# Layer 0's feed forward written in program order, with one work area for several stages

## The chip, the cores and the metric

The kernel runs on one core of a Trainium2 chip. The engines are TensorE (PE: matmuls; its weight loads are shown as PEld), VectorE (DVE), ScalarE (ACT) and GpSimd (POOL); SyncE (SP) issues the DMAs from HBM. Every engine works through its own queue in order; semaphores make one engine wait for another. The metric is the device time of one execution, in microseconds: before the change it is 1958.71, the median of 3 runs that lie between 1958.17 and 1960.01.

## The reference

Two layers over 512 latent and 256 context tokens of width 1024, in fp32, cut here to what the change touches:

```python
def adaln(cond, w_mod, b_mod):
    return jnp.split(jax.nn.silu(cond) @ w_mod + b_mod, N_MOD, axis=-1)     # six vectors of 1024
def swiglu(h, w1, w3, w2):
    return (jax.nn.silu(h @ w1) * (h @ w3)) @ w2                            # D_FF = 2816
def reference(x, c, ctx, c_ctx, w_mod, ...):
    for l in range(2):
        sh1, sc1, gt1, sh2, sc2, gt2 = adaln(c, w_mod[l], b_mod[l])         # for the latent tokens
        csh1, csc1, cgt1, csh2, csc2, cgt2 = adaln(c_ctx, w_mod[l], b_mod[l])   # for the context tokens
        h = modulate(rms_norm(x, norm1[l]), sh1, sc1)
        ... attention, convolution and gMLP branches, each with a gate, summed and projected ...
        x = x + gt1 * merge_branches(...)
        x = x + gt2 * swiglu(modulate(rms_norm(x, norm2[l]), sh2, sc2), w_ff1[l], w_ff3[l], w_ff2[l])
        if l == 0: the same for ctx
    return x
```

## The kernel before

Activations lie transposed: 128 channels on the partitions, the tokens along the free dimension (768 tokens in layer 0, 512 in layer 1). An fp32 product is made of three products of a shorter type: each operand is split into a high part (ACT's cast, L242) and a low part, the difference of the two (on DVE or POOL, L243), and PE adds high x high, high x low and low x high (`mm`, L252). So each 128x512 piece of a weight matrix (256 KB, tile ws, loaded by SP) costs a cast (wh) and a subtraction (wl) before PE can use it. Raw pieces have five slots, high and low parts four each.

Layer 0's feed forward has 22 blocks of 128 hidden channels. Blocks 0 and 1 are made by `first_pair` (L1189). The other twenty are made two at a time by `ff_pair` (L1215): once for w1 (the silu product) and once for w3 (the gate product), each by `pair_product` (L342), a 2 x 2 block product with seven multiplications in place of eight. One multiplication takes one piece of weights and is 12 matmuls of 384 columns (L349). Four of the seven pieces are sums or differences of raw pieces (tile fw, L282 in `factors`), made on DVE; forms of the activations are ready in the tiles A and B. ACT copies intermediate products out of PSUM (tile tp, L358 to L367), DVE forms the outputs of the silu product (L1220 to L1227) and of the gate product (L1234 to L1247), POOL multiplies the two, and `keep_u` splits the result (tile u) for FF2.

The 22 blocks go in five parts: 4, 4, 4, 4 and 6. After each part `ff2_j` (L1270) multiplies its u tiles by eight columns of w2, 24 matmuls for each in the first four parts (512 and 256 columns in turn), and DVE adds the result, times the gate gt2, to the residual (tile xr, L1275).

In the same time DVE computes layer 1's adaln vectors, the sums: 48 pieces of w_mod (512 KB each, tile wm) are multiplied by silu(c), the first sixteen also by silu(c_ctx), and summed along the free dimension (L159). These are 64 operations of 128x1024. `pump` advances them, twice after each pair product and once after every second FF2 block; the load of each (L156) waits for a one-column copy on POOL (`bg_stage`, L183) of a value that the stage has just made, so that a load cannot start long before its stage.

The order of every queue is set by the scheduler of the tile framework, which plans with modelled times; the program's order is only its input. PSUM is used as four banks in two tiles of 1024 columns ("wide") and four single banks ("pD"). Each stage has work tiles of its own (silu output su, tp, fw, score tiles pp, gate tiles: five of 768 columns and two of 512, and others).

## Time and profile before

| | us |
|---|---|
| median of 3 runs | 1958.71 (1958.17 to 1960.01) |
| profiled execution | 1952.57 |
| its span, first to last instruction | 1950.8 |
| PE busy over the span | 1872.5 (96 %) |
| DVE / ACT / POOL busy | 1129.7 / 821.1 / 727.5 |
| PE busy, 0 to 655 us (layer 0 up to the first pair of blocks) | 610.72 |
| PE busy, 655 to 1127 us (layer 0's pairs and the FF2 of the first four parts) | 451.52 of 472.00 |
| PE busy, 1127 us to the end (last FF2 part, layer 1) | 810.27 of 823.80 |

A row of the profile names a line of the kernel, the engine, the operation and its tiles (output, arrow, inputs); x12 is a count. Rows of groups give the busy time, the mean duration in ns, and the idle time of the engine ahead of them with what ended it. In the timeline a row begins with its start and its duration in us, and square brackets hold the idle time before it. A row of waits gives who waited for whom, the total in us, how often, and the longest.

### The profile page before, as it was taken

What the parts mean: (1) busy time and instruction counts of PE and PEld (TensorE: products, weight loads), DVE (VectorE), ACT (ScalarE), POOL (GpSimd) and SP (SyncE); (2) the same over time, 40 slices, a digit from 0 to 9 for tenths busy, and PEclk for the clock granted to TensorE, in tenths of its full rate; (3) what the DMA queues carried; (4) which work ended last, traced back from release to release, by engine and by line L of the source; (5) the groups of instructions that cost most, each with busy time, mean ns of one, the idle gap of its engine ahead of it and who ended that gap; (6) DMA issues with size and microseconds to landing.
All of it is one profiled execution on the core that took longest, in us unless ns stands there. A gap on an engine that the chain in (4) does not pass through costs nothing.

```text
span 1950.8 us, 27784 instructions
## 1 busy us (share of the span) xinstructions
PE 1872.5 (96%) x10146; PEld 1643.3 (84%) x10146; DVE 1129.7 (58%) x1850; ACT 821.1 (42%) x1544; POOL 727.5 (37%) x636
## 2 busy tenths in 40 slices
PE   5999999999999998999999999999999999999999
PEld 4778889888889888888989987888788888888887
DVE  7588877684566877766666657358633461222212
ACT  3547766322225523342433446458533353223231
POOL 4434533332214233333333338654332243233231
PEclk9999999999999999999999999999999999999999
DMA  8653211443443143434343254320133433332333
GB/s 298 225 199 103 71 39 36 136 154 108 147 172 109 55 130 104 134 116 145 122 137 125 71 171 142 105 87 12 34 96 98 140 120 103 97 98 87 108 94 96
DMA packets 109449, 225.58 MB, mean 116 GB/s; under 512 B 12288, under 2 KB 21248, under 8 KB 109184
## 3 DMA queue, kind: packets, MB, share of 16 engines
q1 hardware_dynamic: 108208, 221.96, 35.2%
q10 hardware_dynamic: 1104, 1.84, 0.3%
q8 instruction: 80, 1.31, 0.3%
q14 instruction: 57, 0.47, 0.1%
HBM read 215.89 MB, written 5.24 MB: 113 GB/s over the span
## 4 chain that ended last, share of the span: by engine, by line
PE 76%; DVE 10%; DMA 4%; issue 4%; ACT 3%; POOL 2%; SPq 0%; DVEq 0%; ACTq 0%; POOLq 0%
PE wide L252 29%; PE pD L252 26%; PE pF L252 5%; PE pD L349 5%; PE wide L349 5%; PE pO L1060 2%; DMA wm<-in_w_modT 2%; DMA ws<-in_w 2%; PE wide L1028 2%; PE pPT L1054 2%; DVE wl L243 1%; DVE wm L159 1%; ACT wh L242 1%; DVE nm L1032 1%; DVE fw L282 1%
## 5 line engine op out<-in xcount | busy, mean ns | idle before, releaser
L243 POOL TENSOR_TENSOR wl<-ws,wh 128x512 fp32r<-128x512 f32 (+2 forms) x290 | 382.4, 1321 | 693.2 <-ACT wh L242 682.0
L242 ACT CAST wh<-ws 128x512 fp32r<-128x512 f32 (+2 forms) x534 | 322.4, 607 | 704.6 <-PE wide L252 249.7
L243 DVE TENSOR_TENSOR wl<-ws,wh 128x512 fp32r<-128x512 f32 x244 | 189.6, 780 | 308.2 <-ACT wh L242 305.7
L252 PE MATMUL wide<-A,wh 128*128 128x512 f32 (+2 forms) x1104 | 315.8, 374 | 14.5 <-POOL A L243 5.8
L252 PE MATMUL pD<-A,wh 128*128 128x512 f32 (+1 forms) x1184 | 324.2, 369 | 0.1
L252 PEld LDWEIGHTS wide<-A,wh 128*128 128x128 f32 x1104 | 200.1, 192 | 53.2 <-POOL A L243 7.9
L252 PEld LDWEIGHTS pD<-A,wh 128*128 128x128 f32 x1184 | 207.5, 189 | 38.1 <-POOL A L243 0.3
L252 PE MATMUL pD<-A,wl 128*128 128x512 f32 (+1 forms) x592 | 202.5, 369 | 1.3 <-POOL wl L243 1.3
L252 PE MATMUL wide<-A,wl 128*128 128x512 f32 (+2 forms) x552 | 196.2, 372 | 0.3 <-DVE wl L243 0.3
L252 PE MATMUL wide<-u,wh 128*128 128x512 f32 (+1 forms) x624 | 156.9, 353 | 0.6 <-DVE xr L1275 0.6
L159 DVE SCALAR_TENSOR_TENSOR wm<-wm,fixed 128x1024 f32<-128x1024 f32 x96 | 128.2, 1336 | 35.1 <-DMA wm<-in_w_modT 34.5
L252 PEld LDWEIGHTS pD<-A,wl 128*128 128x128 f32 x592 | 104.3, 188 | 20.7 <-POOL wl L243 2.1
L252 PEld LDWEIGHTS wide<-u,wh 128*128 128x128 f32 x624 | 104.1, 188 | 17.9 <-DVE xr L1275 1.2
L252 PEld LDWEIGHTS wide<-A,wl 128*128 128x128 f32 x552 | 101.9, 192 | 17.7 <-POOL wl L243 0.8
L252 PE MATMUL pD<-u,wh 128*128 128x512 f32 (+1 forms) x432 | 114.6, 358 | 0.0
L1037 POOL TENSOR_SCALAR pp<-pp,nm 128x768 f32<-128x768 f32 (+1 forms) x80 | 69.0, 864 | 106.7 <-DVE nm L1036 87.4
L159 DVE SCALAR_TENSOR_TENSOR junk<-wm,fixed 128x1024 f32<-128x1024 f32 x48 | 64.2, 1338 | 57.6 <-DMA wm<-in_w_modT 57.6
L252 PE MATMUL wide<-u,wl 128*128 128x512 f32 (+1 forms) x312 | 96.2, 353 | 0.1
L252 PE MATMUL pF<-A,wh 128*128 128x256 f32 (+1 forms) x384 | 94.2, 331 | 0.0
L242 ACT CAST wh<-fw 128x512 fp32r<-128x512 f32 x80 | 49.0, 619 | 95.7 <-PE wide L349 26.6
L349 PE MATMUL wide<-B,wh 128*128 128x384 f32 x320 | 81.6, 338 | 5.4 <-ACT wh L242 5.2
L252 PEld LDWEIGHTS pD<-u,wh 128*128 128x128 f32 x432 | 74.2, 188 | 12.3 <-ACT wh L242 0.2
(288 smaller groups left out, 3770.9 us busy)
## 6 DMA issues: line engine op xcount, KB each, us to landing
ws<-in_w SPq DMA_DIRECT2D x256, 256.0 KB, 2.7
wm<-in_w_modT SPq DMA_DIRECT2D x112, 512.0 KB, 4.7
ws<-in_w_in SPq DMA_DIRECT2D x184, 256.0 KB, 2.6
ws<-in_w_o SPq DMA_DIRECT2D x48, 256.0 KB, 2.6
ws<-in_w_abc SPq DMA_DIRECT2D x32, 256.0 KB, 2.6
ws<-in_w_six SPq DMA_DIRECT2D x16, 192.0 KB, 5.2
xr<-in_xT SPq DMA_DIRECT2D x8, 384.0 KB, 8.3
ws<-in_w SPq DMA_DIRECT2D x16, 192.0 KB, 2.3
```

Source lines behind the costliest of these rows:

```text
L159: nc.vector.scalar_tensor_tensor(o, t, 1.0, sbc[:, c, :], op0=ALU.mult, op1=ALU.mult, accum_out=MOD[l][:, sec, b, c:c + 1])
L242: nc.scalar.copy(hi, src)
L243: (lo_eng or nc.gpsimd).tensor_tensor(lo, src, f(hi), op=ALU.subtract)
L252: nc.tensor.matmul(d[:, :b - a], lhsT=ww, rhs=aa[:, a:b], start=kk == 0 and i == 0, stop=kk == n - 1 and i == 2)
L282: nc.vector.tensor_tensor(o, x, y, op=op)
L349: nc.tensor.matmul(D, lhsT=x[:, kk * P:(kk + 1) * P], rhs=a, start=not more and kk == 0 and i == 0, stop=kk == 3 and i == 2, skip_group_ch ...
L1028: nc.tensor.matmul(D[:, a - k0:b - k0], lhsT=q[:, c * P - q0:(c + 1) * P - q0], rhs=kt[:, a:b], start=i == 0, stop=i == 1)
L1032: nc.vector.tensor_reduce(nm[:, 0:1], D[:, :nk], axis=AX.X, op=ALU.max, negate=True)
L1037: nc.gpsimd.tensor_scalar(pt[:, :nk], pt[:, :nk], nm[:, 3:4], 0.0, op0=ALU.mult, op1=ALU.add)
L1054: nc.tensor.transpose(TD[:, (2 * j + cc) * P:(2 * j + cc + 1) * P], pts[cc][:, kc:kc + P], ident)
L1060: nc.tensor.matmul(o[:, 0:256], lhsT=v3[:, kt, :], rhs=pp[:, j * 256:(j + 1) * 256], start=gi == 0 and j == 0 and i == 0, stop=gi == len(k ...
```

## The change

`ff_layer_0` holds all of layer 0's feed forward from the second pair to the last; its body stands in `tc.manual_schedule()`, in which every queue runs in the order of the program. The first pair, the FF2 of the last part and all other stages are ordered by the scheduler as before.

- `flow` takes the place of `factors` and `taken`: one stream of pieces for pairs and FF2 alike, made three ahead of their use. A raw load is issued when the piece that last used its slot has been made. The low parts of FF2 pieces are all made on DVE; before, some of them were made on POOL.
- The sums of layer 1 come at fixed steps: at the third multiplication of each pair product (EXTRA), after the FF2 blocks 2 to 7 of the first two parts, and after every FF2 block of the next two. A sum's load is issued three steps ahead, into a ring of four, with no copy on POOL.
- `behind` delays a silu or a `keep_u` by one or two pieces in the program's order.
- FF2 of a part starts with the two older u tiles for column 0, then for column 1, then the two newer ones for both.
- PSUM is eight single banks in rotation (pE) within `ff_layer_0`.
- One tile `work` of 9472 columns holds rings for the sums, score tiles (pp), gate tiles (six), su, tp, fw and a tile of the first stage; some rings share columns. Two u tiles of each part lie in unused halves of the A tiles. Some tiles are merged or moved (q and qc, pt, wx, wb), and the homes of A and B are swapped for layer 1.

The matmuls and their number are the same (10066 instructions on PE's queue in both). DVE has 16 instructions more, POOL 64 fewer (48 of them the copies). The diff, cut to its core:

```diff
+    work = const.tile([P, 9472], F32, name="work")
+    RINGS = {"sums": (0, 1024, 4), "turned": (4096, 2560, 1), "pp": (0, 1536, 3), "gate": (4864, 768, 6),
+             "su": (4096, 768, 2), "tp": (5632, 384, 6), "fw": (7936, 512, 3)}
+    place = dict.fromkeys(RINGS, 0)
+    place["gate"] = 3
+    def area(name, n=None):
+        a, w, bufs = RINGS[name]
+        i = place[name]
+        place[name] = (i + 1) % bufs
+        return work[:, a + i * w:a + i * w + (n or w)]
...
     def wm_stage():
-        return wp.tile([P, 1024], F32, tag="wm", name="wm", bufs=3)
+        return area("sums")
+    def spare(skip=2):
+        i = (place["sums"] + skip) % 4 * 1024
+        return work[:, i:i + 1024]
...
+    ahead_sums = []
+    sums_1 = iter([(sec, b, (0, 1) if sec < 2 else (0,)) for sec in (1, 0, 2, 4, 3, 5) for b in range(KD)])
+    def load_1():
+        x = next(sums_1, None)
+        if x:
+            t = wm_stage()
+            nc.sync.dma_start(t, w_modT[1, x[0] * KD + x[1]])
+            ahead_sums.append((*x, t))
+    def sums_layer_1():
+        if ahead_sums:
+            sec, b, cs, t = ahead_sums.pop(0)
+            for c in cs:
+                o = t if c == cs[-1] else spare(0)
+                nc.vector.scalar_tensor_tensor(o, t, 1.0, sbc[:, c, :], op0=ALU.mult, op1=ALU.mult,
+                                               accum_out=MOD[1][:, sec, b, c:c + 1])
+            if b == KD - 1:
+                mod_rest(1, sec, 0, KD, 0, len(cs))
+            load_1()
...
-    def factors(srcs):
-        def load(n, b, k0):
-            if n == len(srcs):
-                return None
-            t = wtile("s")
-            nc.sync.dma_start(t, srcs[n][b][:, k0:k0 + 4, :].rearrange("p k n -> p (k n)"))
-            return t
-        def parts(x, eng=nc.vector):
-            hi, lo = wtile("h"), wtile("l")
-            split(x, hi, lo, eng)
-            return hi, lo
-        def total(x, y, op):
-            o = slot("fw", 512)
-            nc.vector.tensor_tensor(o, x, y, op=op)
-            return o
-        nxt = [load(0, *i) for i in ((0, 0), (1, 0), (1, 4), (0, 4))] + [load(1, 0, 0)]
-        for n in range(len(srcs)):
-            a11, a21, a22, a12, *nxt = nxt
-            yield parts(a11, nc.gpsimd)
-            s1 = total(a21, a22, ALU.add)
...
+    def flow(items, ahead=3):
+        n_s, loads, raw, todo = 5, [], [], []
+        def need(src, last):
+            loads.append((src, last))
+            return len(loads) - 1
+        for pair, x in items:
+            t0 = len(todo)
+            if not pair:
+                i = need(x, t0)
+                todo.append((lambda i=i: raw[i], nc.vector))
+                continue
+            a11, a21, a22, a12 = (need(x[b][:, k0:k0 + 4, :].rearrange("p k n -> p (k n)"), t0 + last)
+                                  for b, k0, last in ((0, 0, 4), (1, 0, 4), (1, 4, 6), (0, 4, 5)))
+            s = {}
+            def total(name, p, q, op, s=s):
+                def go():
+                    o = s[name] = area("fw")
+                    u, v = (raw[i] if isinstance(i, int) else s[i] for i in (p, q))
+                    nc.vector.tensor_tensor(o, u, v, op=op)
+                    return o
+                return go
+            todo += [(lambda i=a11: raw[i], nc.gpsimd), (total("s1", a21, a22, ALU.add), nc.vector),
+                     (total("s2", "s1", a11, ALU.subtract), nc.vector), (total("s4", "s2", a12, ALU.subtract), nc.vector),
+                     (total("s3", a11, a21, ALU.subtract), nc.vector), (lambda i=a12: raw[i], nc.vector),
+                     (lambda i=a22: raw[i], nc.vector)]
+        made, summed, count = [], [], [0, 0]
+        def issue():
+            while len(raw) < len(loads) and (len(raw) < n_s or loads[len(raw) - n_s][1] < count[0]):
+                t = wtile("s")
+                nc.sync.dma_start(t[:, :loads[len(raw)][0].shape[1]], loads[len(raw)][0])
+                raw.append(t)
+        def sums():
+            if count[1] < len(todo):
+                summed.append(todo[count[1]][0]())
+                count[1] += 1
+        def make():
+            if summed:
+                x, (_, eng) = summed.pop(0), todo[count[0]]
+                hi, lo = wtile("h"), wtile("l")
+                split(x, hi, lo, eng)
+                made.append((hi, lo))
+                count[0] += 1
+                issue()
+        issue()
+        sums()
+        def take(as_is=False):
+            while not as_is:
+                sums()
+                make()
+                if len(made) > ahead or not summed:
+                    break
+            for w in waiting:
+                w[0] -= 1
+            while waiting and waiting[0][0] <= 0:
+                waiting.pop(0)[1]()
+            return made.pop(0)
         return take
+    waiting = []
+    def behind(n, what):
+        waiting.append([n, what])
...
-    def pair_product(take, tmp, ev11, ev12, ev21, ev22):
+        return [area(name) for i in range(4)]
+    def pair_product(take, tmp, ev11, ev12, ev21, ev22, extra):
+        step = [0]
         def prod(D, right, more=False):
             wh, wl = take()
+            step[0] += 1
+            if step[0] == EXTRA:
+                extra()
...
+        spot = [2]
         def keep_u(su, U):
-            hi, lo = two("u", W)
+            i = len(U) - spot[0]
+            if last or i not in (0, 1):
+                hi, lo = two("u", W)
+            else:
+                hi, lo = (arena[4 * i + 1 + 2 * j][:, :NT] for j in range(2))
             split(su, hi, lo)
             U.append((hi, lo))
...
             def silu22(x, y):
                 nc.vector.tensor_tensor(b2, x, y, op=ALU.subtract)
-                nc.scalar.activation(b2, b2, AF.Silu)
+                behind(1, lambda: nc.scalar.activation(b2, b2, AF.Silu))
             def silu11(x, D):
                 nc.vector.tensor_tensor(a1, x, D, op=ALU.add)
-                nc.scalar.activation(sa, sa, AF.Silu)
+                behind(1, lambda: nc.scalar.activation(sa, sa, AF.Silu))
...
             def mul11(x, D):
                 nc.vector.tensor_tensor(x, x, D, op=ALU.add)
                 nc.gpsimd.tensor_tensor(a1, a1, x, op=ALU.mult)
-                keep_u(sa, U)
+                behind(2, lambda: keep_u(sa, U))
             def mul21(D):
                 nc.vector.tensor_tensor(b1, b1, D, op=ALU.mult)
-                keep_u(sb, U)
-            pair_product(take, four("tp"), silu11, silu12, silu21, silu22)
-            pump(2)
-            pair_product(take, four("tp"), mul11, mul12, mul21, mul22)
-            pump(2)
+                behind(1, lambda: keep_u(sb, U))
+            pair_product(take, four("tp"), silu11, silu12, silu21, silu22, sums_layer_1)
+            pair_product(take, four("tp"), mul11, mul12, mul21, mul22, sums_layer_1)
+        def ff_layer_0(parts):
+            items = []
+            for f0, f1 in parts:
+                items += [(True, w_13[l, i, 2 * m:2 * m + 2]) for m in range(f0 // 2, f1 // 2) if m for i in range(2)]
+                if f1 < NFF:
+                    items += [(False, w_2[l, j][:, f0:f1, :].rearrange("p k n -> p (k n)")) for j in range(KD)]
+            U = []
+            first_pair(U)
+            with tc.manual_schedule():
+                for _ in range(3):
+                    load_1()
+                take = flow(items)
+                for pi, (f0, f1) in enumerate(parts):
+                    if pi:
+                        U, spot[0] = [], 0
+                    for m in range(f0 // 2, f1 // 2):
+                        if m:
+                            ff_pair(m, U, take)
+                    if f1 == NFF:
+                        while waiting:
+                            waiting.pop(0)[1]()
+                        return U
+                    w, D = {}, {}
+                    def some(j, ks):
+                        if j not in w:
+                            wh, wl = take(j == 1)
+                            w[j] = [(wh[:, i:i + P], wl[:, i:i + P]) for i in range(0, 512, P)]
+                            D[j] = [next_bank() for _ in segs]
+                        for k in ks:
+                            mm(D[j], w[j][k:k + 1], U, segs, k=k)
+                    for j in range(KD):
+                        if j == 0:
+                            some(0, (0, 1))
+                            some(1, (0, 1))
+                            some(0, (2, 3))
+                        else:
+                            some(j, range(4) if j > 1 else (2, 3))
+                        if j >= 2 or pi > 1:
+                            sums_layer_1()
+                        for d, (a, b) in zip(D[j], segs):
+                            c = int(a >= SEQ)
+                            nc.vector.scalar_tensor_tensor(X[j][:, a:b], d[:, :b - a], MOD[l][:, 5, j, c:c + 1],
+                                                           X[j][:, a:b], op0=ALU.mult, op1=ALU.add)
         parts = [(0, 8), (8, 15), (15, 22)] if last else [(0, 4), (4, 8), (8, 12), (12, 16), (16, 22)]
+        if not last:
+            U = ff_layer_0(parts)
+            new_wide()
+            parts = parts[-1:]
         for pi, (f0, f1) in enumerate(parts):
-            U = []
             if last:
+                U = []
                 plain(f0, f1, U)
-            else:
-                ms = range(f0 // 2, f1 // 2)
-                take = taken(factors([w_13[l, i, 2 * m:2 * m + 2] for m in ms if m for i in range(2)]))
-                for m in ms:
-                    if m:
-                        ff_pair(m, U, take)
-                    else:
-                        first_pair(U)
             if f1 == NFF and not last:
+                homes[0] = "BA"
                 hnext = new_h()
             def ff2_j(j, sg):
                 w = load_w(w_2[l, j][:, f0:f1, :], f1 - f0)
@@ -1275,9 +1420,6 @@
                     nc.vector.scalar_tensor_tensor(X[j][:, a:b], D, MOD[l][:, 5, j, c:c + 1],
                                                    X[j][:, a:b], op0=ALU.mult, op1=ALU.add)
                 gemm(w, U, sg, ev)
-                if not last and f1 < NFF:
-                    gate_mods[0] = X[j][:, W - 1:W]
-                    pump(j % 2)
```

Three places in the queues, as the two programs have them (line, operation, output, inputs, shape; the lines are those of each kernel, and work is the shared tile).

DVE in the silu product of blocks 14 and 15, in the fourth part. Before:

```order
L243 TENSOR_TENSOR wl<-ws,wh 128x512 x2
L1220 TENSOR_TENSOR su<-tp,pD 128x384
L159 SCALAR_TENSOR_TENSOR wm,fixed<-wm,fixed 128x1024
L1227 TENSOR_TENSOR su<-tp,wide_73 128x384
L159 SCALAR_TENSOR_TENSOR wm,fixed<-wm,fixed 128x1024
L243 TENSOR_TENSOR wl<-fw,wh 128x512
L159 SCALAR_TENSOR_TENSOR wm,fixed<-wm,fixed 128x1024
L282 TENSOR_TENSOR fw<-fw,ws 128x512
```

And in the changed kernel:

```order
L341 TENSOR_TENSOR work<-ws 128x512
L295 TENSOR_TENSOR wl<-work,wh 128x512 x2
L295 TENSOR_TENSOR wl<-ws,wh 128x512
L243 SCALAR_TENSOR_TENSOR work,fixed<-work,fixed 128x1024
L295 TENSOR_TENSOR wl<-ws,wh 128x512
L1323 TENSOR_TENSOR work<-work,pE 128x384
L341 TENSOR_TENSOR work<-ws 128x512
L1326 TENSOR_TENSOR work<-work 128x384
```

Three sums stood within five instructions there, around the outputs of the silu product (L1220, L1227); now one sum (L243) stands ahead of them in a whole pair product.

SP's queue around the same place. Before:

```order
L156 DMA wm<-in_w_modT 128x1024 x2
L272 DMA ws<-in_w 128x512 x2
L156 DMA wm<-in_w_modT 128x1024 x3
L272 DMA ws<-in_w 128x512 x9
L156 DMA wm<-in_w_modT 128x1024 x2
```

And in the changed kernel:

```order
L353 DMA ws<-in_w 128x512 x4
L234 DMA work<-in_w_modT 128x1024
L353 DMA ws<-in_w 128x512 x4
L234 DMA work<-in_w_modT 128x1024
L353 DMA ws<-in_w 128x512 x6
```

The loads of sums came in groups of up to three between the loads of weight pieces; now they come singly.

PE at the start of the first part's FF2 in the changed kernel, the first row of each stretch (j = 0 has the banks pE_6264 and pE_6265, j = 1 pE_6278 and pE_6279; u_5884 and u_5990 are the high parts of the older u tiles, A_5066 that of a newer one):

```order
L304 MATMUL pE_6264<-u_5884,wh_160 128x512
L304 MATMUL pE_6265<-u_5884,wh_160 128x256
...
L304 MATMUL pE_6264<-u_5990,wh_160 128x512
...
L304 MATMUL pE_6278<-u_5884,wh_160 128x512
...
L304 MATMUL pE_6278<-u_5990,wh_160 128x512
...
L304 MATMUL pE_6264<-A_5066,wh_160 128x512
```

Both columns use the older u tiles first, 24 matmuls; before, each column of w2 went through its four u tiles before the next column.

92 lines of the change are left out of this document (47 added, 45 removed).

## The prediction

> **What bounds the kernel now.** I read the busy times by stretch first, for layer 0's feed forward from its first pair product to the end of its FF2 before the last part, then the same stretch for the lines of the pair products alone (columns: the stretch, its length, PE busy, PEld, DVE, ACT, POOL, granted clock, DMA share, GB/s; in the second row PE and PEld only).
>
> ```profile
> 655.00:1127.00 472.00, 451.52 (x2523) 420.98 (x2522) 329.32 (x501) 172.52 (x312) 153.97 (x136) 1.00 0.36 117
> 655.00:1127.00 472.00, 304.46 (x1680) 290.72 (x1680) 1.00 0.36 117
> ```
>
> TensorE is busy for 451.5 of 472.0 us and no other engine for more than 329.3, so TensorE's work and its waits make this stage. A busy row can hide pipelined slack, so I take TensorE's pace from the chain of waits, where it runs without a wait.
>
> ```profile
> 918.60 8.48 PE wide L252 x48
> 962.27 4.16 PE pD L349 x24
> 735.29 3.81 PE wide L349 x12
> ```
>
> A matmul of 384 columns comes every 4.16/24 = 0.1733 us; those of FF2 (512 and 256 columns in turn) every 8.48/48 = 0.1767 us. Of the 2523 matmuls, 1680 are pair products and about 50 the end of the first pair (384 columns too); 793 are FF2. At full pace that is 1730 x 0.1733 + 793 x 0.1767 = 299.8 + 140.1 = 439.9 us. The stage loses 472.0 - 439.9 = 32.1 us. The third row is the same product at 0.317 us a matmul: 1.7 us lost behind one long wait, at a lowered clock.
>
> Next the waits of PE, then those of DVE and of SP's queue, in this stretch (total, times, longest).
>
> ```profile
> PE wide L349 <- ACT wh L242: 5.6, 7, 1.6
> PE wide L349 <- DVE xr L1275: 5.4, 2, 4.4
> PE pD L349 <- ACT wh L242: 3.2, 6, 1.1
> PE pD L349 <- ACT tp L361: 1.8, 1, 1.8
> PE wide L349 <- DVE su L1203: 0.9, 1, 0.9
> DVE wm L159 <- DMA wm<-in_w_modT: 34.5, 14, 7.5
> DVE junk L159 <- DMA wm<-in_w_modT: 22.3, 6, 8.8
> SPq L156 <- POOL wm L183: 90.2, 35, 11.0
> ```
>
> PE's waits name ACT and DVE: nearly all are for a piece of weights (wh), or for a bank that an evacuation (xr) has not emptied. Three rows of short waits (wl 1.4, tp 1.0, another xr 0.6) are not shown; with them the sum is 19.9 us. Behind DVE stands the DMA of the adaLN sums (wm), which SP issues only after POOL's gate copy. The timeline shows the whole chain once, at 970:
>
> ```profile
> 970.85 2.70 SPq L156 DMA_DIRECT2D wm<-in_w_modT  x3
> 975.61 1.23 DVE L159 SCALAR_TENSOR_TENSOR wm<-wm,fixed 128x1024 f32<-128x1024 f32 x1 [3.71 <-DMA wm<-in_w_modT]
> 976.76 0.55 DVE L1227 TENSOR_TENSOR su<-tp,wide 128x384 f32<-128x384 f32 x1
> 977.34 0.84 ACT L1228 ACTIVATE su<-su 128x768 f32<-128x768 f32 x1 [3.89 <-DVE su L1227]
> 978.09 0.60 ACT L242 CAST wh<-fw 128x512 fp32r<-128x512 f32 x1
> 978.75 0.99 PE L349 MATMUL wide<-B,wh 128*128 128x384 f32 x4 [1.62 <-ACT wh L242]
> ```
>
> DVE stands 3.71 us before a sum whose load left late. The silu product's addition (L1227) is behind it, ACT's silu behind that, the cast of the next piece behind the silu, and PE waits 1.62. The longest wait has the same cause:
>
> ```profile
> 717.96 7.63 SPq L156 DMA_DIRECT2D wm<-in_w_modT  x2
> 732.35 0.69 DVE L282 TENSOR_TENSOR fw<-ws 128x512 f32<-128x512 f32 x1 [2.21 <-DMA ws<-in_w]
> 735.29 0.61 PE L349 MATMUL wide<-A,wh 128*128 128x384 f32 x2 [4.44 <-DVE xr L1275]
> ```
>
> SP's queue holds two gated sum loads over 7.63 us; the piece behind them reaches DVE late (2.21), and the FF2 evacuation that frees PE's bank stands behind that piece: 4.44 us, and then the slow product above.
>
> **The change part by part.** The order of the queues is now the program's. A sum's load is issued three sums ahead without POOL's copy, and the steps of the sums are fixed. The rows that price it, grouped over the same stretch (busy, mean ns, idle before):
>
> ```profile
> L243 DVE TENSOR_TENSOR wl<-fw,wh 128x512 fp32r<-128x512 f32 x80 | 60.5, 760 | 11.5 <-ACT wh L242 11.2
> L159 DVE SCALAR_TENSOR_TENSOR wm<-wm,fixed 128x1024 f32<-128x1024 f32 x48 | 60.4, 1259 | 34.5 <-DMA wm<-in_w_modT 34.5
> L159 DVE SCALAR_TENSOR_TENSOR junk<-wm,fixed 128x1024 f32<-128x1024 f32 x16 | 20.6, 1287 | 22.3 <-DMA wm<-in_w_modT 22.3
> L243 DVE TENSOR_TENSOR wl<-ws,wh 128x512 fp32r<-128x512 f32 x60 | 48.8, 823 | 11.7 <-ACT wh L242 11.7
> L282 DVE TENSOR_TENSOR fw<-ws 128x512 f32<-128x512 f32 x39 | 36.1, 925 | 11.8 <-DMA ws<-in_w 11.6
> L282 DVE TENSOR_TENSOR fw<-fw,ws 128x512 f32<-128x512 f32 x39 | 29.4, 755 | 12.8 <-DMA ws<-in_w 12.5
> L1275 DVE SCALAR_TENSOR_TENSOR xr<-wide,fixed,xr 128x512 f32<-128x512 f32 x22 | 16.3, 742 | 5.7 <-PE wide L252 5.7
> L1275 DVE SCALAR_TENSOR_TENSOR xr<-pD,fixed,xr 128x256 f32<-128x256 f32 x10 | 4.7, 471 | 0.0
> L1238 DVE TENSOR_TENSOR tp<-tp 128x384 f32<-128x384 f32 x10 | 12.5, 1250 | 8.2 <-ACT tp L367 8.2
> L1234 DVE TENSOR_TENSOR tp<-tp,wide 128x384 f32<-128x384 f32 x10 | 5.5, 548 | 4.8 <-PE wide L349 4.8
> wm<-in_w_modT SPq DMA_DIRECT2D x112, 512.0 KB, 4.7
> ```
>
> *DVE as a whole.* Sixteen subtractions of FF2 pieces come over from POOL: 16 x 0.82 = 13.2, so DVE holds 329.3 + 13.2 = 342.5 us against 439.9 of PE. It stays the second engine with 97 us to spare. POOL loses them and 48 copies.
>
> *DVE in a pair product.* PE needs 7 x 12 x 0.1733 = 14.56 us. DVE makes seven pieces: two sums from raw pieces at 0.925 and two at 0.755 = 3.36, four low parts at 0.760 and two at 0.823 = 4.69. The silu product adds three operations of 0.55 (1.65), the gate product three such and one of 1.25 (2.90). A sum step adds 1.26, or 2.55 where both conditionings are summed (the first 16). The dearest case is 3.36 + 4.69 + 2.90 + 2.55 = 13.5, and with one conditioning 12.2: both fit under 14.56. The piece is three products ahead, 3 x 2.08 = 6.24 us, so an operation that is a few us late does not reach PE.
>
> *The sum loads.* A sum's load is issued three steps before its use. Two steps of a pair are 14.56 us apart, those of FF2 blocks 24 x 0.1767 = 4.24. The shortest lead is 3 x 4.24 = 12.7 us against 4.7 us to landing: DVE's 56.8 us of waits on wm go, and with them the chains shown above. SP's waits behind POOL (90.2) go too. If that cover failed, the price is that of the slower rival below.
>
> *What stays.* (a) The start: PE's first products of A wait for the first pair's last evacuation, whose chain is the same (0.9 above, and a few short waits that the scheduled part still orders): 2 us. (b) The start of FF2 in each part. The last two u tiles come out of this chain:
>
> ```profile
> L1243 POOL TENSOR_TENSOR su<-su,tp 128x384 f32<-128x384 f32 x10 | 13.5, 1348 | 79.6 <-DVE tp L1242 79.6
> L242 ACT CAST u<-su 128x768 fp32r<-128x768 f32 x21 | 17.5, 836 | 25.5 <-DVE su L1247 11.4 <-POOL su L1243 10.4 <-POOL su L1235 3.4
> L243 POOL TENSOR_TENSOR u<-su,u 128x768 fp32r<-128x768 f32 x21 | 39.2, 1864 | 35.5 <-ACT u L242 35.5
> ```
>
> From the end of the product before the last (2.08 us before the last ends, at T): 0.55 on DVE, 1.35 and two times 1.86 on POOL with ACT's 0.84 between: -2.08 + 0.55 + 1.35 + 0.84 + 3.73 = T + 4.4. Two blocks of FF2 begin with the two older u tiles, 24 matmuls or 4.24 us, and reach the last low part at about 4.24 + 1.41 = T + 5.65. The cover is 1.2 us. If DVE is one product (2.08) late, each of four part ends costs 0.9: I take 1 for the four together, of 0 to 4. (c) The ends of FF2 in parts 0 and 1, where sums of both conditionings fall on FF2 blocks. DVE needs 0.82 + 0.74 + 0.47 + 2.55 = 4.58 a block by the means, PE 4.24; over six blocks DVE falls 2.0 us behind. With the last evacuation (1.21) and the next piece's two operations (1.69) that is 4.9 against the 6.24 of pieces in hand. It is covered by 1.3, less the small accumulator reads between the sums, which I have not counted. I take 1, of 0 to 3. (d) Irregular collisions on DVE and POOL that no view shows as waits: 12.2 of the 32.1 us are not in listed waits, 1.7 of it is the slow clock; I take 2 as staying, of 0 to 10.
>
> How far DVE's prices swing is seen in one operation in the same stretch, alone and beside a POOL subtraction:
>
> ```profile
> 658.85 0.68 DVE L282 TENSOR_TENSOR fw<-ws 128x512 f32<-128x512 f32 x1
> 668.82 2.03 POOL L243 TENSOR_TENSOR u<-su,u 128x768 fp32r<-128x768 f32 x1 [11.31 <-ACT u L242]
> 669.07 2.32 DVE L282 TENSOR_TENSOR fw<-ws 128x512 f32<-128x512 f32 x1
> ```
>
> The Trainium skill, SBUF — State Buffer, section Who interferes with whom, says that a DVE instruction with two SBUF inputs and a GpSimd instruction that reads SBUF exclude each other, and that an evacuation with one SBUF input does not. The trace agrees: the second addition ends 0.54 us after the POOL row. By that rule, with POOL empty during FF2, the DVE work of a block would be at its uncontended prices and (c) would be 0, one us less; and the gate product, whose five POOL operations remain, would be the place that runs late.
>
> Stage: 32.1 - 2 - 1 - 1 - 2 = 26 us gained.
>
> *Around it.* The gate tiles of the attention stages get a ring of six in one work area. In layer 1 the end of attention has bubbles that gate products can fill:
>
> ```profile
> 1320.00:1392.00 72.00, 67.51 (x464) 58.05 (x463) 63.84 (x135) 57.09 (x113) 27.41 (x29) 1.00 0.03 8
> ```
>
> 4.5 us idle here; with more gate tiles, matmuls that now run after attention run inside. Bounds 0 and 4.5; I take 2, nearer the middle, since DVE is as busy as 63.8 of 72 there. Merged tiles, the two swapped homes and the moved weight tiles change no instruction's size: nothing, their waits lie under PE's other work; bounds -5 to 5, as no row shows the new sharing.
>
> Sum: 26 + 2 = 28. The profiled execution took 1952.57 us, so 1924.6; the median of the runs shown, 1958.71, is 6.1 above it: 1924.6 + 6.1 = 1930.7 us.
>
> **The rivals.** *A. Only the sums' waits go, DVE runs late in the products.* For it: 13.5 against 14.56 leaves one us a product, and one collision of the kind shown costs 1.6. If half a us stays in each of the 20 products (10) with all of (b) (4) and (a) (2), 16 stay and 16 are gained, none in attention: 1942.7. Against it: two thirds of the steps are at 12.2 or less, and the lead of pieces is 6.24. *B. In-order DVE is blocked by sums: slower.* The place is the fixed sum step in program order: if the load is not there, all of DVE's queue waits, with the next piece and the evacuations. Before, 20 such waits averaged 56.8/20 = 2.8 us. If each of the 48 steps waited 2.8 us, DVE would need 342.5 + 134 = 477, 5 above the 472 of now: 1963.7. It decides from 97/48 = 2.0 us a step, and from 2.7 a step the kernel is slower. For it: SP's queue is in order too, and a piece's load that waits for its slot holds the sum's load. Against it: 12.7 us of lead against 4.7. *C. The gain is given back in the scheduled stages*, whose score tiles, gates and sums now lie in one area: no change, 1958.7. For it only that the trace shows no row of it; against it that 28 us would have to appear elsewhere, while the one stretch of attention that I show idles for 4.5 of 72 now. That the change doesn't do what it says is excluded by the order of the queues.
>
> **How the numbers follow.** Forecast 0.66, A 0.18, B 0.07, C 0.05, and 0.04 that all 32 us and 5 more go, 1921 or less. The forecast's own range: with (b) and (c) at 4 and 3 and nothing in attention it gains 28 - 5 - 2 = 21 (1938); with (b), (c) and (d) at 0 and 4.5 in attention 28 + 4 + 2.5 = 34.5 (1924). To hold 8 in 10 I go to A's side, 1946, and on the other to 1919 (nothing stays but (a), and all 4.5 of the attention: 30.1 + 4.5 = 34.6, and the unknown 5 of the new sharing). About 0.2 %, 3.9 us, is what a measurement of this kernel tells from no change. Forecast, A and the last case are faster: 0.88; C 0.05; B 0.07.
>
> **What would show it.** In the new profile the stretch from the first pair product to the end of FF2 before the last part should be about 446 us with PE waits under 6 us in all; DVE's waits for the sums' DMA near zero and SP with no wait on POOL; DVE busy about 340. The step on (b) fails if PE waits for u at FF2's start, the step on the products if PE waits for wh in most products, (c) if a wait follows the FF2 of part 0 or 1. B shows as DVE waiting for in_w_modT. The prediction is wrong if that stretch is longer than 460 us, or if the time outside it moves by more than 5 us.

## The result: 1930.9 us, a ratio of 0.9856

The changed kernel takes 1930.89 us (median of 4 runs, 1928.51 to 1932.14); the kernel before 1958.47 (4 runs, 1958.17 to 1960.01). The ratio is 0.9856, with a 95% interval of 0.9839 to 0.9873: 27.6 us less. The forecast was 1930.7. The profiled execution took 1930.93 us, so it stands for its runs; that of the kernel before, at 1952.57 us, was quicker than any of its timed runs, and the experiments come back to it.

### The profile page after: what moved, and what is told of

It reads as the page before. It is cut to its first block, busy times and chain, and to the rows that moved or that the text cites. A ratio compares the mean times of both kernels' runs of the same rounds, so it can differ in the third digit from the quotient of the medians.

```text
span 1929.1 us, 27661 instructions
## 1 busy us (share of the span) xinstructions
PE 1866.0 (97%) x10146; PEld 1647.7 (85%) x10146; DVE 1143.4 (59%) x1866; ACT 823.4 (43%) x1544; POOL 702.4 (36%) x572
## 4 chain that ended last, share of the span: by engine, by line
PE 55%; DVE 3%; ACT 1%; issue 1%; POOL 1%; DMA 0%; ACTq 0%; DVEq 0%; POOLq 0%
PE pD L304 17%; PE wide L304 16%; PE pE L435 12%; PE pE L304 5%; PE pF L304 2%; PE pO L1157 1%; PE pPT L1150 1%; PE wide L1124 1%; DVE nm L1128 1%; POOL u L295 0%; DVE ny L495 0%; DVE pt L1154 0%; ACT work L1131 0%; DVE B L500 0%; DVE nacc L471 0%
## 5 line engine op out<-in xcount | busy, mean ns | idle before, releaser
L295 POOL TENSOR_TENSOR wl<-ws,wh 128x512 fp32r<-128x512 f32 (+2 forms) x274 | 364.4, 1333 | 745.5 <-ACT wh L294 704.1
L295 DVE TENSOR_TENSOR wl<-ws,wh 128x512 fp32r<-128x512 f32 x260 | 199.8, 770 | 311.9 <-ACT wh L294 309.5
L304 PE MATMUL wide<-B,wh 128*128 128x512 f32 (+1 forms) x816 | 230.6, 372 | 4.5 <-DVE B L500 1.9
L304 PE MATMUL pD<-B,wh 128*128 128x512 f32 (+1 forms) x720 | 218.4, 384 | 0.1
L304 PE MATMUL wide<-A,wh 128*128 128x512 f32 (+2 forms) x608 | 162.2, 360 | 13.4 <-POOL A L295 6.6
L304 PEld LDWEIGHTS wide<-B,wh 128*128 128x128 f32 x816 | 144.9, 189 | 33.1 <-DVE B L500 2.5
L435 PE MATMUL pE<-B,wh 128*128 128x384 f32 x640 | 162.6, 334 | 1.1 <-ACT work L444 1.0
L304 PEld LDWEIGHTS pD<-B,wh 128*128 128x128 f32 x720 | 134.1, 189 | 26.4 <-POOL B L295 0.3
L304 PE MATMUL wide<-B,wl 128*128 128x512 f32 (+1 forms) x408 | 143.8, 373 | 0.1
L304 PE MATMUL pD<-B,wl 128*128 128x512 f32 (+1 forms) x360 | 138.0, 384 | 0.0
L304 PE MATMUL pD<-A,wh 128*128 128x512 f32 (+1 forms) x544 | 130.6, 349 | 0.1
L435 PE MATMUL pE<-A,wh 128*128 128x384 f32 x480 | 121.8, 334 | 0.0
L304 PEld LDWEIGHTS pD<-A,wh 128*128 128x128 f32 x544 | 88.4, 189 | 14.8 <-ACT wh L294 0.4
L295 DVE TENSOR_TENSOR wl<-work,wh 128x512 fp32r<-128x512 f32 x80 | 80.7, 1014 | 15.8 <-ACT wh L294 15.7
```

The source lines that it names most:

```text
L295: (lo_eng or nc.gpsimd).tensor_tensor(lo, src, f(hi), op=ALU.subtract)
L304: nc.tensor.matmul(d[:, :b - a], lhsT=ww, rhs=aa[:, a:b], start=kk == 0 and i == 0, stop=kk == n - 1 and i == 2)
L435: nc.tensor.matmul(D, lhsT=x[:, kk * P:(kk + 1) * P], rhs=a, start=not more and kk == 0 and i == 0, stop=kk == 3 and i == 2, skip_group_ch ...
```

## The profile after

The page's head:

```profile
span 1929.1 us, 27661 instructions
PE 1866.0 (97%) x10146; PEld 1647.7 (85%) x10146; DVE 1143.4 (59%) x1866; ACT 823.4 (43%) x1544; POOL 702.4 (36%) x572
```

The busy times of the stretch from just ahead of the first pair product to the end of the last (columns as in the prediction, whose stretch of 472 us also ends with the last pair product, not with the FF2 before the last part as its words have it):

```profile
658.00:1098.00 440.00, 438.14 (x2513) 419.76 (x2513) 339.91 (x516) 174.73 (x312) 114.37 (x71) 1.00 0.38 122
```

440 us in place of 472, with PE busy for all but 1.9. The waits in this stretch are all of PE's, the longest of DVE's, and SP's for the sums' slots:

```profile
PE pE L435 <- ACT work L444: 1.0, 1, 1.0
PE pE L304 <- POOL u L295: 0.7, 2, 0.4
...
DVE wl L295 <- ACT wh L294: 35.4, 39, 1.4
DVE xr L1400 <- PE pE L304: 32.1, 19, 5.0
...
SPq L234 <- DVE work L243: 62.8, 24, 5.7
```

19.9 us of PE's waits have become 1.7. DVE's waits on the DMA of the sums are gone from the list; DVE now waits for PE (L1400, the FF2 evacuation), which means that it is ahead. SP waits for a slot that a sum (L243) has to leave, not for POOL. The sums themselves (L243), between the low parts of the sums of raw pieces (L295) and the additions of raw pieces (L341), by form:

```profile
L295 DVE TENSOR_TENSOR wl<-work,wh 128x512 fp32r<-128x512 f32 x80 | 80.7, 1014 | 15.8 <-ACT wh L294 15.7
L243 DVE SCALAR_TENSOR_TENSOR work<-work,fixed 128x1024 f32<-128x1024 f32 x64 | 79.0, 1234 | 0.6
L341 DVE TENSOR_TENSOR work<-ws 128x512 f32<-128x512 f32 x39 | 28.9, 742 | 0.0
```

64 sum operations stand idle for 0.6 us in all; before it was 34.5 + 22.3.

To compare all runs by place I took from each trace the starts of the matmuls: the time from one start to the next, less the usual spacing for its columns (0.173 us for 384, 0.227 for 512, 0.119 for 256, 0.109 for 128), is PE's loss. It holds PE's waits and also what a lowered granted clock costs. Both kernels hold the same matmuls (10146 records in each trace, 1818.9 us at these spacings), so losses can be set side by side at equal work done: up to the feed forward (540 us of work), its first pair (to 600; this reaches some 16 us into the pair products), pairs and FF2 (to 1050), layer 1's start (to 1120), layer 1's attention (to 1500). Behind that no run loses anything.

| loss of PE, us | to 540 | first pair | pairs, FF2 | layer 1 start | layer 1 attention | time of this execution |
|---|---|---|---|---|---|---|
| before, the prediction's profile | 48.3 | 8.9 | 33.1 | 4.1 | 19.5 | 1952.57 |
| before, once more | 49.4 | 8.9 | 37.5 | 4.0 | 19.5 | 1958.06 |
| before, no sums | 51.3 | 9.3 | 9.1 | 4.1 | 18.2 | 1930.99 |
| before, no copies on POOL | 47.6 | 57.2 | 11.2 | 5.3 | 17.8 | 1978.11 |
| changed | 52.0 | 8.2 | 3.6 | 7.3 | 21.4 | 1930.93 |
| changed, once more | 52.0 | 8.2 | 3.1 | 5.4 | 23.0 | 1930.23 |
| changed, no sums | 51.3 | 8.3 | 0.9 | 4.2 | 21.1 | 1924.34 |
| changed, sums loaded one step ahead | 51.3 | 8.2 | 5.2 | 4.2 | 21.1 | 1928.70 |
| changed, sums loaded at their step | 51.0 | 8.2 | 56.0 | 4.3 | 21.1 | 1979.52 |
| changed, ordered by the scheduler | 52.0 | 58.9 | 8.6 | 5.5 | 21.5 | 1985.38 |
| changed, FF2 in plain order | 49.5 | 8.3 | 10.7 | 5.5 | 22.9 | 1935.72 |
| changed, nothing delayed by `behind` | 49.8 | 8.2 | 29.2 | 7.0 | 21.1 | 1954.10 |
| changed, homes not swapped | 51.0 | 8.2 | 2.5 | 7.0 | 21.2 | 1928.66 |
| changed, two gate tiles in layer 1 | 52.3 | 8.2 | 3.6 | 6.2 | 21.4 | 1930.58 |

Each row is one execution, profiled and timed, save that the changed kernel and the one before were also timed as above. In the two profiles of the changed kernel the column of pairs and FF2 differs by 0.5 us; layer 1's start and attention differ by 1.9 and 1.6, which goes with the granted clock, as will be shown.

The second profile of the changed kernel was taken to see which of its losses outside the pairs come back. The expectation was that those of the layout come back within 1 us and that chance ones go, with a total 2 to 4 us off 1930.9. The total was 0.7 off; layer 1's start lost 1.9 less and its attention 1.6 more, so that run alone decided nothing.

## The experiments

**The kernel before, once more.**

> The kernel before, unchanged, profiled once more. Its first profiled execution took 1952.57 us, its timed runs 1958.2 to 1960.0. If that one execution was a quick one, this one takes 1957 to 1960 and the missing 5 to 6 us show as more loss in some stretch of the trace; if profiled executions are quicker as such, it takes about 1952.5 again.

1958.06 us: the first profiled execution was a quick one. Of the 5.5 us between them 4.4 lie in the pairs and FF2, the very place that the change rewrites. Most of this is the granted clock (the last number but two): in that stretch it stood at 0.50 for 3.4 us in the first profile (the first row here) and for 10.2 us in the second (the other two), and 6.8 us more at half speed are worth about 3:

```profile
735.80:739.20 3.40, 3.40 (x12) 3.40 (x11) 1.24 (x3) 0.33 (x1) 1.28 (x3) 0.50 0.55 199
```

```profile
734.70:741.50 6.80, 5.45 (x17) 5.45 (x18) 3.93 (x9) 1.00 (x2) 1.72 (x3) 0.50 0.57 186
983.90:987.30 3.40, 3.40 (x12) 3.40 (x12) 3.40 (x7) 1.42 (x3) 0.00 (x0) 0.50 0.00 0
```

Further runs of the kernel before beside the experiments took 1960.0, 1960.5 and 1955.5.

**Sums taken out of both kernels.** The edits, in the kernel before and in the changed one:

```diff
-                    mod_sums(l, sec, b, cs, bg_stage())
+                    if l == 0:
+                        mod_sums(l, sec, b, cs, bg_stage())
...
-            nc.sync.dma_start(t, w_modT[1, x[0] * KD + x[1]])
-                nc.vector.scalar_tensor_tensor(o, t, 1.0, sbc[:, c, :], op0=ALU.mult, op1=ALU.mult,
```

> The kernel before without layer 1's sums: their 48 loads, 48 copies on POOL and 64 operations on DVE are left out (the adaln vectors of layer 1 are zeros in their place); everything else is unchanged and ordered by the scheduler. Theory (late gated sum loads stop in-order DVE, and ACT and PE behind it): the feed forward's stretch loses under 10 us in place of 32, the total is 20 to 27 us shorter than before. Rival (the scheduler's order of pieces and evacuations loses the time, with or without sums): the stretch still loses over 22 us, the total falls by less than 10.

> The changed kernel without layer 1's sums (loads and DVE operations left out, vectors zero). Theory (with program order and loads three ahead the sums are hidden completely): the feed forward's stretch loses 4 us as now, the total changes by less than 2. Rival (DVE is near its limit in the products, and the rest of the loss is the sums'): the stretch loses nothing and the total falls by 3 to 5.

The waits of PE in the pairs and FF2 of the kernel before without sums (all of them):

```profile
PE wide L351 <- ACT wh L244: 2.5, 4, 1.1
PE pD L351 <- ACT tp L363: 1.0, 1, 1.0
PE wide L351 <- DVE su L1205: 0.9, 1, 0.9
```

The loss there falls from 33 to 37 us to 9.1, the total by 27 against the run before on the same measure (1958.06): the theory's range. So in the kernel before the sums cost 24 to 28 us, and 9.1 stay without them. In the changed kernel the sums cost 2.2 to 2.7 (3.1 and 3.6 against 0.9). That is nearer to that run's rival, by which the stretch loses nothing without them, than to its theory, by which they are hidden completely. Without sums the two kernels lose 9.1 and 0.9; which of their other differences (the order of the queues, FF2's order, the rings) make these 8 us is not shown by this pair of runs. The total of the changed kernel without sums fell by 6.6, more than the theory's 2 and the rival's 3 to 5: 3.1 of it is at layer 1's start, where the granted clock fell in the one execution and not in the other (last section).

**The loads set free in the kernel before.**

```diff
-        if gate_mods[0] is not None:
+        if l == 0 and gate_mods[0] is not None:
             nc.gpsimd.tensor_copy(t[:, 0:1], gate_mods[0])
```

> The kernel before with one part of the change alone: the loads of layer 1's sums no longer wait for POOL's copies (48 copies gone); sums, slots and the scheduler stay. Theory (the loads come late because of the gate): DVE's 57 us of waits on them fall below 20 and the total by 12 to 20 us. Rival (the scheduler's order puts loads and sums badly with or without the gate): DVE still waits over 35 us, the total falls by less than 5.

18 to 20 us slower, which neither theory expected. The stretch around the first pair, and the pairs behind it:

```profile
560.00:686.00 126.00, 99.13 (x510) 91.55 (x509) 118.47 (x202) 44.78 (x84) 39.20 (x23) 0.86 0.63 224
686.00:1153.00 467.00, 450.08 (x2523) 424.40 (x2522) 273.98 (x409) 174.95 (x312) 129.62 (x88) 0.98 0.27 84
```

The sums by form, two rows of the first stretch and the one of the second:

```profile
L159 DVE SCALAR_TENSOR_TENSOR wm<-wm,fixed 128x1024 f32<-128x1024 f32 x34 | 44.3, 1309 | 0.1
L159 DVE SCALAR_TENSOR_TENSOR junk<-wm,fixed 128x1024 f32<-128x1024 f32 x20 | 25.4, 1269 | 1.4 <-DMA wm<-in_w_modT 1.4
...
L159 DVE SCALAR_TENSOR_TENSOR wm<-wm,fixed 128x1024 f32<-128x1024 f32 x19 | 24.9, 1319 | 0.6 <-DMA wm<-in_w_modT 0.6
```

And PE's longest wait in the first:

```profile
PE wide L252 <- ACT A L242: 9.9, 2, 6.8
```

Of layer 1's 64 sum operations only 19 are left in the pairs; 54, a few of layer 0's among them, stand around the first pair. They fill DVE (118.5 of 126 us) just where it must form layer 0's normed activations (A), and PE waits: 57.2 us lost against 8.9. Not all of it is waiting. The busy times between the matmuls that bound this column of the table, in the kernel before and in this one:

```profile
602.70:671.50 68.80, 62.97 (x354) 59.51 (x354) 60.79 (x90) 41.22 (x78) 27.50 (x19) 1.00 0.21 66
```

```profile
602.10:719.30 117.20, 77.78 (x355) 70.76 (x354) 114.31 (x192) 42.16 (x78) 32.00 (x17) 0.78 0.59 201
```

PE is idle for 39.4 us there in place of 5.8, and its busy time is 14.8 us longer for the same matmuls, at a granted clock of 0.78 in place of 1.00. In the pairs behind, only 11.2 are lost. So the copies on POOL did two things: they kept the sums away from that place, and made them late where they were.

**The changed kernel under the scheduler.**

```diff
-            with tc.manual_schedule():
+            if True:
```

> The changed kernel with the feed forward given back to the scheduler: the same program text, work area, pieces three ahead, sums at the same steps and loaded three ahead without POOL's copy, but the order of the queues is the scheduler's. Theory A (program order is what keeps the sums in their places; the kernel before without POOL's gate lost 47 us ahead of the feed forward because its sums were pulled to the front): the total grows by more than 20, with DVE's sums in a heap early. Theory B (loads ahead and pieces ahead suffice, whoever orders): the total grows by less than 8.

The same happens: 40 sums before 684 us, 58.9 lost around the first pair, 8.6 in the pairs (9.1 in the kernel before without sums). The group of the sums ahead of 684 us, and PE's longest wait there:

```profile
L243 DVE SCALAR_TENSOR_TENSOR work<-work,fixed 128x1024 f32<-128x1024 f32 x40 | 54.8, 1378 | 0.1
```

```profile
PE wide L304 <- ACT A L294: 16.4, 2, 10.7
```

Theory A holds. In both kernels in which the scheduler had the loads without the copies, it put the sums in front of the first pair, and the loss there was larger than what the pairs gained.

**How far ahead the loads must be.** For a lead of one, `range(3)` becomes `range(1)`; for none, it becomes `range(0)` and the load moves from the end of its step to the start:

```diff
     def sums_layer_1():
+        load_1()
         if ahead_sums:
...
-            load_1()
...
-                for _ in range(3):
+                for _ in range(0):
                     load_1()
```

> The changed kernel with each sum's load issued at its own step in place of three steps ahead; all else as changed. This tests the price of the slower rival. Theory (an in-order DVE stands at each sum until its load lands): with 4.7 us to landing and most of that waited at 48 steps DVE needs 342 + 48 x 4 = 534 us, so the stretch grows from 440 to about 530 and the total to about 2020; DVE waits for the sums' DMA about 190 us in all. Rival (SP's queue runs ahead of DVE, so the load is early anyway): DVE waits under 40 us, the total moves by less than 10.

> The changed kernel with each sum's load issued one step ahead, between the three steps of the change and the none of the run that cost 49 us. Theory (what counts is whether the lead covers the landing): in the pairs a step lies 14.6 us ahead, in FF2 blocks 4.24 against 4.7 to landing, so only FF2 steps wait, 28 of them by about 0.5 us, which the pieces in hand cover: total within 3 us of 1930.5, DVE's waits on the sums under 15 us. Rival (three steps are needed because SP's queue holds a load behind pieces that wait for slots): DVE waits over 40 us, 10 us or more are lost.

The stretch with no lead:

```profile
658.00:1150.00 492.00, 458.43 (x2510) 431.93 (x2509) 347.48 (x515) 173.03 (x311) 114.48 (x72) 0.96 0.34 112
```

DVE's wait and the three longest of PE in it:

```profile
DVE work L244 <- DMA work<-in_w_modT: 107.6, 35, 6.1
...
PE pE L435 <- ACT work L444: 11.8, 10, 2.0
PE pE L435 <- DVE xr L1400: 8.6, 4, 3.6
PE pE L435 <- DVE wl L295: 7.5, 5, 2.2
```

DVE's wait with a lead of one:

```profile
DVE work L243 <- DMA work<-in_w_modT: 8.3, 9, 1.8
```

With no lead 35 sums wait 3.1 us each on average, and PE's chain is again DVE, ACT, PE: 52.4 us are lost against the lead of three. PE is idle for 33.6 of the 492 us; a granted clock of 0.96 over the whole stretch is worth about 20 more (an estimate, 0.04 of 492). The mechanism is the theory's, its size is not: the waits are fewer and shorter than expected (107.6 us for 190), and the total is 1979.5, not 2020, so part of the landing is covered even then. With a lead of one step nine short waits remain, and in the pairs and FF2 1.6 to 2.1 us more are lost than with three; the total, 1928.70, is not longer. So the lead needed is about one step, as expected from the landing time; the second and third are margin.

**FF2 in plain order.**

```diff
-                            wh, wl = take(j == 1)
+                            wh, wl = take()
...
-                        if j == 0:
-                            some(0, (0, 1))
-                            some(1, (0, 1))
-                            some(0, (2, 3))
-                        else:
-                            some(j, range(4) if j > 1 else (2, 3))
+                        some(j, range(4))
```

> The changed kernel with the FF2 of each part in plain order: column 0 through its four u tiles before column 1. Theory (the last u tiles come at T + 4.4 us after the last product; column 0 now wants their low parts at T + 2.5 and T + 3.5, one on the heels of the other): a wait of PE for u on POOL of 1 to 2 us at four starts, total 4 to 8 us longer. Rival (the last u tiles are ready early, the order of FF2 hides nothing): within 2 us.

```profile
PE pE L304 <- POOL u L295: 5.4, 6, 1.6
PE pE L304 <- POOL A L295: 1.2, 2, 0.8
```

Eight waits of PE for the low parts of u, two at each of the four starts (in the first part these u tiles lie in A's tiles, so the row names A), and 7.1 to 7.6 us lost: the theory's 4 to 8. The chain of step (b) is about as long as reckoned, and the interleaved order covers it but for 0.7.

**Nothing delayed.**

```diff
     def behind(n, what):
-        waiting.append([n, what])
+        what()
```

> The changed kernel in which silu, gate product and split of u stand in the program right behind the output of their product, not one or two pieces later. Theory (in-order ACT then stands before the silu while the cast of the next pieces waits behind it): pieces are three ahead, so PE sees little of it: 0 to 4 us longer, the loss as waits for wh in the pair products. Rival (the delay is what keeps ACT's casts in time): over 8 us longer.

25.6 to 26.1 us more are lost in the pairs and FF2: the rival. The prediction had not priced `behind` at all. PE's longest wait there, by its total:

```profile
PE pE L435 <- ACT work L444: 16.1, 6, 3.4
```

The timeline of this kernel at one gate product, all engines, other rows left out:

```profile
759.90 1.39 POOL L1346 TENSOR_TENSOR work<-work 128x384 f32<-128x384 f32 x1 [1.09 <-DVE work L1345]
761.32 0.84 ACT L294 CAST A<-work 128x768 fp32r<-128x768 f32 x1 [5.09 <-POOL work L1346]
762.06 0.61 ACT L294 CAST wh<-work 128x512 fp32r<-128x512 f32 x1
762.71 1.90 DVE L295 TENSOR_TENSOR wl<-work,wh 128x512 fp32r<-128x512 f32 x1 [2.29 <-ACT wh L294]
764.53 0.54 DVE L1350 TENSOR_TENSOR work<-work,pE 128x384 f32<-128x384 f32 x1
765.11 0.83 ACT L294 CAST A<-work 128x768 fp32r<-128x768 f32 x1 [2.43 <-DVE work L1350]
766.36 0.47 ACT L444 COPY work<-pE 128x384 f32<-128x384 f32 x1
766.88 0.45 PE L435 MATMUL pE<-B,wh 128*128 128x384 f32 x1 [3.37 <-ACT work L444]
```

ACT stands 5.09 us before the split of u, because POOL's product is not there; the next piece's cast is behind it, DVE's low part behind the cast (2.29), DVE's output of the last product (L1350) behind that, ACT's second split behind that, and the copy that empties PE's bank (L444) last: 3.37 us. It happens in five of the ten gate products (the sixth wait of the row, 1.1 us, stands at the start, as in the changed kernel). The clock adds to it: from 762 to 772 us the granted clock was 0.83, in the changed kernel 1.00. In the changed kernel the same two splits wait 0.2 us each. It is the chain of the prediction with another head: an instruction that waits in an in-order queue, and casts behind it.

**Layer 1.**

```diff
-                homes[0] = "BA"
+                homes[0] = "AB"
...
+        if last:
+            RINGS["gate"], place["gate"] = (4864, 768, 2), 0
```

> The changed kernel without the swap of the two homes for layer 1: layer 1's normed activations go to A's tiles again, of which some hold u until the last FF2 has read them. Theory (the swap removes a wait at layer 1's start): layer 1's start loses 3 to 8 us more. Rival (the homes do not matter): within 1.5 us there.

> The changed kernel with two gate tiles in rotation in layer 1 in place of six (layer 0 keeps six). In layer 1's attention both profiles of the changed kernel lose some 22 us from the first projection to the output projection, both of the kernel before 20; the prediction had named the longer ring as a gain there. Theory A (with six tiles the gate products run earlier and leave the end of attention without filler): the loss falls back by 2 to 3 us. Theory B (the merged query and probability tiles or the scheduler's new plan cost it): it stays within 1 us. If the longer ring is a gain as predicted, it grows.

In the second kernel two gate tiles are fewer than the gates that live at once, so some gate values are overwritten; the instructions are the same, but not all the waits between them. Its layer 1 attention loses 21.4, as the changed kernel's (21.4 and 23.0), which is theory B: the ring's length alone neither gains nor costs there. It is not the ring of the kernel before, where each gate tile was a tile of its own. Without the swap of homes layer 1's start loses 7.0, not 3 to 8 more than the changed kernel's 7.3: the rival. The two compare, since from 1145 to 1165 us both had a granted clock of 0.83. So no gain of the swap is seen.

## Why the prediction was right, and where it was not

*The cause.* Late sum loads in front of in-order DVE, then ACT, then PE: shown, by the removal of the sums (24 to 28 us of 33 to 37) and by the dose (no lead 56.0, one step 5.2, three steps 3.6 lost). DVE's busy time was given as 342.5 us in this stretch; it is 339.9. But its parts did not keep their prices: the 80 low parts of the sums of raw pieces went from 0.760 to 1.014 us (20.2 us more in all), and the 78 additions that make these sums became cheaper (10.1 us less). What the prediction lacked is that the change needs three things together: the early load, the fixed order and `behind`. Without fixed order the sums go to the front (58.9 lost there), and without `behind` ACT takes DVE's place as the engine that stands (29.2). I had read the order of the queues as a means to early loads; it is a condition of its own.

*The stage.* 26 of 32.1 us were to go, and the stretch was to take 446 us; it takes 440. By matmul starts 33.1 fell to 3.6, so 29.5 went. What stays is smaller at (a) to (c): (a) 1.0 us of waits, not 2 (it stands at 672 us, so the table counts it with the first pair); (b) 0.7, not 1; (c) none, not 1. The rest, (d), is 2 to 3 us where 2 was taken; the prediction gave no reason for that figure, so this agreement is luck. For (c) the sentence on the Trainium skill, SBUF — State Buffer, section Who interferes with whom, was the better guide: with POOL nearly empty in FF2 the same subtraction takes 0.68 us, in the pair products 1.04. The trace agrees over the whole stretch: of these 80 subtractions, the 58 that overlap no POOL row take 0.68 to 0.69 us, the 22 that overlap one 1.88 on average. The other half of what the prediction worked out from it, that the gate product would be the place that runs late, did not show: PE waits nowhere in it. The rows are of FF2 of the first part and of the pair products behind it:

```profile
L295 DVE TENSOR_TENSOR wl<-work,wh 128x512 fp32r<-128x512 f32 x2 | 1.4, 684 | 0.0
...
L295 DVE TENSOR_TENSOR wl<-work,wh 128x512 fp32r<-128x512 f32 x14 | 14.4, 1037 | 2.4 <-ACT wh L294 2.2
```

In FF2's stretch POOL (the fifth busy time) works for 4.70 of 31.5 us:

```profile
699.00:730.50 31.50, 31.50 (x184) 27.77 (x183) 25.78 (x44) 4.79 (x9) 4.70 (x3) 1.00 0.40 126
```

*Around the stage.* A gain of 2 in layer 1's attention was named; against the same profile 8.1 us were lost outside the stage: 3.0 up to the first pair product, 3.2 at layer 1's start, 1.9 in attention. Against the second profile of the kernel before it is 7.1. The prediction had called itself wrong if the time outside moved by more than 5 us; by this sign of its own, its part on the surroundings failed, though the total came out. The 3.2 at layer 1's start are the granted clock: where it stayed at 1.00 the changed kernel lost 4.2 (no sums, and a lead of one), as the kernel before did. The attention step failed: every kernel with the new layout loses 21.1 to 23.0 there, every one with the old 17.8 to 19.5. The upper ends of both ranges are executions in which the clock stood at 0.50 for 3.4 us late in attention (both profiles of the kernel before, the second of the changed one, FF2 in plain order); without these it is 21.1 to 21.5 against 17.8 to 18.2, so the new layout costs about 3 us. The ring's length is not the cause. What is (merged query and probability tiles, or the scheduler's plan for them), stays open. The first stretch (49.5 to 52.3 against 47.6 to 51.3) and layer 1's start (4.2 to 7.3 against 4.0 to 5.3) overlap between old and new.

*From the profile to the median.* I added 6.1 us, the distance of the profiled execution from its median, as if it were the same after. It was not: that execution had been quick in the very stretch that was rewritten (33.1 lost; 37.5 in the second profile), and after the change little is left there to vary (3.6 and 3.1). So the forecast of 1930.7 came out of three terms that were off and cancelled: against the first profile -26 - 2 + 6.1 = -21.9, measured -29.5 + 8.1 = -21.4. That it hit within 0.2 us is luck. The executions of the kernel before lie between 1952.57 and 1960.53 us, 8 us apart, where the prediction took 3.9 us as what can be told from no change.

*The rivals.* A (DVE late in the products) did not come: PE's waits for a piece are gone from the list. B did not come either, but its mechanism is real, and its price was too low. By its formula DVE at 342.5 + 107.6 = 450 us would have cost 10 over PE's 440; it cost 52.4, some 20 of it by the lowered clock, for which the formula has no term. So the slack of DVE does not act as one pool of 97 us: a wait of 3.1 us can exceed what the product at hand has. That is argued from these totals, not shown product by product. C is the 8.1 us above, under a third of the 28 it needed.

## What to carry to other kernels

Ask of every instruction in an in-order queue what it waits for and what stands behind it; a load, a silu or a split that waits on a slower engine belongs behind the casts that feed TensorE. Freeing a load from its gate without fixing its order can be worse than the gate: look where a scheduler will then put the work. Take the offset between a profiled execution and the median over to a changed kernel only if it lies outside the part that changes, and profile the kernel before twice to know. Read the granted clock beside each loss before you put the loss down to a layout.

## What the runs showed of the hardware

The granted clock fell after much shorter waits than the 4.44 us of the prediction. At layer 1's start in the changed kernel two waits of PE, 0.83 and 1.00 us, two microseconds apart, were the only ones in the six microseconds ahead of it:

```profile
1151.08 0.50 PE L304 MATMUL wide<-B,wh 128*128 128x512 f32 x1 [0.83 <-POOL B L295]
1153.06 0.79 PE L304 MATMUL wide<-B,wh 128*128 128x512 f32 x1 [1.00 <-DVE B L500]
```

The busy times by stretch (the last number but two is the granted clock):

```profile
1150.00:1155.00 5.00, 3.16 (x10) 2.04 (x9) 5.00 (x6) 3.82 (x7) 5.00 (x4) 0.80 0.48 144
1155.00:1160.00 5.00, 5.00 (x16) 4.09 (x15) 2.00 (x3) 0.71 (x2) 5.00 (x5) 0.52 0.54 161
1160.00:1165.00 5.00, 5.00 (x24) 4.10 (x23) 0.55 (x1) 1.15 (x2) 2.58 (x3) 1.00 0.18 52
```

PE is busy throughout 1155 to 1160 at about half speed, which costs some 2.4 us. The traces record where the clock changes: here it stood at 0.50 from 1153.0 to 1159.8 us, 6.8 us. In all fourteen traces it is either 1.00 or 0.50, and each stretch at 0.50 ahead of the last matmul lasts 3.4 us or a whole multiple of it, up to 27.3.

The same two waits do not always cost the same. In the second profile they were 0.82 and 1.02 us, and the clock stood at 0.50 for 3.4 us (0.91 over 1145 to 1165); with a lead of one step, a kernel with the same instructions here, they were 0.71 and 1.02 us, and it stayed at 1.00. Layer 1's start lost 7.3, 5.4 and 4.2 us in these three. So one to three of the microseconds that lie between executions are the clock's, and what decides whether it falls is not shown.
